# Two orders moved in a Strassen decoder trunk: where partial products are copied and finished in the second feed-forward entry, and in which order attention's two accumulators leave PSUM

## The chip, the cores and the metric

The kernel runs on one NeuronCore of one Trainium2 chip. The metric is the device time of one execution in microseconds. Smaller is better.

The engines are named as the profile names them: PE is TensorE's matrix multiply (PEld its weight loads), DVE is VectorE, ACT is ScalarE, POOL is GpSimd, and SP is SyncE, which issues most of the loads. Each of them works through its own list of instructions in order; an instruction that waits for a semaphore holds up everything behind it on the same engine.

## The reference

The program is a decoder trunk of two layers over 1024 positions and 1024 channels, all in float32. Layer 0 mixes by a short gated convolution, layer 1 by dilated attention with three branches; a SwiGLU feed-forward with 2816 hidden channels follows each. Cut to what matters here:

```
for i in range(2):
    h = rms_norm(x, mix_norm[i])
    x = x + (short_conv_mixer(h, ...) if i == 0 else dilated_attention_mixer(h, ...))
    h = rms_norm(x, ffn_norm[i])
    x = x + (silu(h @ w_gate[i]) * (h @ w_up[i])) @ w_down[i]
return rms_norm(x, final_norm)

# dilated attention: 16 heads of 64, q, k, v from one projection
s = q . k * 64**-0.5 + bias(distance), masked to the branch's band
o, lse = softmax(s) @ v, logsumexp(s)            # for each of three branches
o = sum(softmax(lse over branches) * o); x = x + o @ w_out
```

## The kernel before

**Precision.** A float32 operand is split into a high part (a copy rounded to the fast matmul type, made by ACT, line 139 or 567) and a low part (the rest, made by DVE, line 140 or 568). A product then takes three matmuls: high by high, high by low, low by high (lines 369 to 371 in plain products, 575 to 577 in the Strassen ones). Low parts of the weights are read by lines 371 and 577 alone.

**Feed-forward.** The gate and up projections are done by Strassen's scheme in Winograd's form: a unit `u` is one pair of 128-channel tiles, and instead of eight block products it takes seven, `(u, m)` with `m` from 1 to 7. Each product is 12 matmuls of 128x512. Gate units are even, up units odd. The order in which the products stand is a table (`unit_order`). In the second feed-forward (`key` 1) it begins `(0,1) (1,1) (2,1) (3,1) (0,2) (1,2) (2,2) (3,2) (4,1) (4,2) (0,6) (1,6) (0,7) (1,7) (0,4) (1,4) (0,5) (1,5) (0,3) (1,3) (2,6) (2,5) (2,7)`, numbered from 0, and goes on with units 3, 4 and so forth. One bank of PSUM, `p`, takes products 1, 6, 7 and 4 of a unit one upon the other; after 1, 6 and 7 ACT copies the bank out as a partial sum (line 581, tile `part`), and the next product of the unit must wait for that copy. Another bank, `r`, takes products 5 and 3; between the two DVE adds it to a saved partial (line 585). A third, `q`, holds product 2 until it is added to the saved product 1 (`first`, line 585). So the four quarters of a unit come out: `(0,0)` is the plain sum of products 1 and 2, the others need more. For a finished quarter ACT takes the SiLU (line 1239, gate units), DVE multiplies (line 1242, up units), POOL stores it.

**Operands of the second half.** The seven sums of activation blocks that the products read (tiles `b`) are made while the first products run, since they need the norm of the second 512 columns. `second_half` is a generator: each `next` makes one more piece. Its steps are: sums for product 7 and, at the following `next`, 6; a subtraction (`hcol<-hcol,x`); high and low parts for product 4, with a scaling (`x<-x,rstd`); a subtraction (`hcol<-x`); high and low parts for product 5 (`b<-hcol`); high and low parts for product 3 (`b<-x`). `start(n)` runs behind product number `n` and, at the numbers in a table, takes one such step after it has asked for the weights of product `n + 3` (`ensure`).

**Attention.** The heads are handled one a slot, 16 slots and one more to drain. Slot `n` computes the scores of head `n` (matmuls of line 1503 and 1504 into a fresh bank of PSUM each, read by DVE) and beside them the values of head `n - 1` (`values`, line 1579): small matmuls, in 14 pieces, into two accumulators, `acc[0]` for the first 512 positions and `acc[1]` for the second. ACT copies each accumulator out as 64 rows of denominators (`z`, line 1598) and 64 rows of outputs (`o`, line 1599). Dense projections of other heads are laid between. In odd slots ACT then splits the next pair's keys and queries (`split_kq`, line 1472), and at the end of each slot it takes the exponentials (line 1566; the first is tile `lf`), which the values of the next slot read. PSUM has 8 banks; a freed bank goes to the next one that asks, and the order of all instructions on each engine is fixed as the program is written.

**The end of attention.** For the last pair, `finish` turns the denominators into factors by logarithm and exponential, scales each half of the output and splits it, while `ensure` prepares the weights of the output projection (`ahead_ao` is the place of its third tile, counted from 0 as tile 2).

Of the kernel before, what the change touches and what calls it, by code (L numbers as in the profile page):

```python
# [24 lines left out]
NPAIR = H // 2  # L25
# [65 lines left out]
def view(t, off, dims):  # L91
    return bass.AP(tensor=t.tensor, offset=t.offset + off, ap=[t.ap[0]] + [list(d) for d in dims])
# [3 lines left out]
def trunk(ctx: ExitStack, tc: tile.TileContext, x, gains_in, cwi, ck, cwo, wqkv, wo, relb,  # L96
# [8 lines left out]
    def page(name, dt=F32):  # L105
        return pages.tile([128, 1024], dt, name=name, tag="page", bufs=PAGES)
# [6 lines left out]
    def bank():  # L113
        return psum.tile([128, 512], F32, name="bank", tag="bank")

    def half(h):
        return slice(h * HALF, (h + 1) * HALF)
# [45 lines left out]
    def ensure(upto):  # L163
        while op_state[0] < min(upto + 1, len(ops)):
            key = ops[op_state[0] + 1][0] if op_state[0] + 1 < len(ops) else None
            if key in sums_of:
                sums_of.pop(key)()
            if op_state[0] not in made:
                made[op_state[0]] = ops[op_state[0]][1]()
            op_state[0] += 1  # L170

    def take(key, ahead=1):
        i = op_state[1]
        assert ops[i][0] == key, (ops[i][0], key)
        ensure(i + ahead)
        op_state[1] += 1
        return made.pop(i)
# [196 lines left out]
    def run(*gens):  # L374
        for _ in zip(*gens):
            pass
        for g in gens:
            for _ in g:
                pass
# [6 lines left out]
    def both(w, ks, acts):  # L386
        banks = two_banks()
        run(product(w, ks, acts, banks))
        return banks
# [114 lines left out]
    def add_to_x(n, banks):  # L504
        for (c0, c1), b in banks.items():
            nc.vector.tensor_tensor(out=X[n][:, c0:c1], in0=X[n][:, c0:c1], in1=b[:, :c1 - c0], op=ALU.add)  # L506
# [34 lines left out]
    class Strassen:  # L541
# [75 lines left out]
        def whole(self, u, m, d):  # L617

            if m == 1:
                d["p"] = self.bank()  # L620
            elif m in (2, 5):
                d["q" if m == 2 else "r"] = self.bank()
            self.mm((u,), m, d["q" if m == 2 else "r" if m in (5, 3) else "p"], m in (1, 2, 5))
            if m in (1, 6, 7):
                d[{1: "u1", 6: "u2", 7: "u3"}[m]] = self.save(d["p"])
            if (u, m) == (0, 6):
                self.first(0)
            if m == 4:
                self.out(u, (1, 0), d.pop("p"))
            elif m == 3:  # L630
                self.out(u, (0, 1), self.add(d.pop("u2"), d.pop("r")))
            elif m in (5, 7) and "u3" in d and "r" in d:
                self.out(u, (1, 1), self.add(d.pop("u3"), d["r"]))
            early = self.key != 0
            if m == 2 and u > 3 + early or (u, m) in ((0, 4), (3, 7)):
                for x in {0: range(4), 3: (4,) * early}.get(u, (u,)):
                    self.out(x, (0, 0), self.first(x))
                    del self.st[x]["u1"]

# [506 lines left out]
    class Swiglu(Strassen):  # L1146
# [100 lines left out]
        def feed_forward(self, stats, last_step, after, final=None):  # L1247
            prep = []

            def start(n):  # L1250
                if n == 0:
                    last_step()
                    if not self.key:
                        for m in (6, 7):
                            combos[self.key, 1](m)
                        ensure(self.at(3, 1))
                if n == 1 + self.key:
                    next(stats)
                if n == 1:
                    if self.key:  # L1260
                        for m in (6, 7):
                            combos[self.key, 1](m)
                    ensure(self.at(0, 6))
                if n == 2 + 2 * self.key:
                    run(stats)
                    prep.append(self.second_half())
                    next(prep[0])
                    nc.scalar.activation(scratch, eps, AF.Silu)
                if n == 2:
                    ensure(self.at(1, 6))  # L1270
                elif n == 4:
                    ensure(self.at(1, 7))
                if n in ((5, 7, 8, 9, 11), (5, 6, 9, 10, 11, 15))[self.key]:
                    ensure(self.base + n + 3)
                    next(prep[0], None)

            self.run(start)
            key = ("d", self.key)
            if final:
                final(key, self.plain, self.hid)  # L1280
                return
            for n in range(KT):
                add_to_x(n, both(take(key + (n,)), self.plain, self.hid))
                after(n)
# [95 lines left out]
    def blk(j):  # L1380
        return (j // 4) * HALF + (j % 4) * 8

    def attention(norm):
# [185 lines left out]
        def values(p, a, st):  # L1569
            lf, lh, ld, lp = (st[n] for n in ("lf", "lh", "ld", "lp"))  # L1570
            o, z = st["o"], st["z"]
            n0 = slice(64 * a, 64 * a + 64)
            z0 = slice(64 - 64 * a, 128 - 64 * a)
            acc = [bank(), bank()]
            kd = [[128, 4], [1, 32]]
            b1 = [[32, 16], [1, 8]]

            def mm(ih, off, dims, u, rhs, first=False, last=False):
                nc.tensor.matmul(view(acc[ih], off, dims), vx[:, u, 64 * a:64 * a + 128], rhs,  # L1579
                                 start=first, stop=last)  # L1580

            for ih in range(2):
                for r4 in range(4):
                    mm(ih, r4 * 32, kd, 8 + r4, view(lf, ih * HALF + r4 * 32, kd), first=r4 == 0)
                    if r4 % 2:
                        yield
            for r4 in range(4):
                mm(1, r4 * 32, kd, 12 + r4, view(lh, r4 * 32, kd))
                if r4 % 2:
                    yield  # L1590
            for j in range(8):
                off = (j % 4) * 8
                mm(j // 4, off, b1, j, view(ld, blk(j), b1), last=False)
                if j:
                    mm(j // 4, off, b1, j - 1, view(lp, blk(j), b1), last=j % 4 == 3)
                if j % 4 == 3:
                    ih, s = j // 4, half(j // 4)
                    nc.scalar.activation(z[n0, s], acc[ih][z0], AF.Copy)
                    nc.scalar.activation(o[n0, s], acc[ih][n0], AF.Copy)
                yield  # L1600

        def finish(p):

            o, z = OZ.pop(p)
            if p < NPAIR - 1:
                zd, rd = zdram[p]
                nc.sync.dma_start(zd, z[0:65:64])
                yield
                zc = scope["pool"].tile([128, 16], F32, name="zc", tag="zc", bufs=2)
                nc.sync.dma_start(zc, bass.AP(zd.tensor, zd.offset, [[16, 128], [1, 16]]))  # L1610
                yield
                nc.vector.reciprocal(zc, zc)
                nc.sync.dma_start(bass.AP(rd.tensor, rd.offset, [[16, 128], [1, 16]]), zc)
                yield
                nc.sync.dma_start(z, bass.AP(rd.tensor, rd.offset, [[S, 2], [0, 64], [1, S]]))
                yield
                put_off.append((p, o, z))
                return

            acts[p] = page("o_hi", F32R), page("o_lo", F32R)  # L1620

            def scaled(c0, c1):
                q = slice(c0, c1)
                nc.vector.tensor_tensor(out=o[:, q], in0=o[:, q], in1=z[:, q], op=ALU.mult)

            def parts(h):
                split(o[:, half(h)], [t[:, half(h)] for t in acts[p]])

            nc.scalar.activation(z, z, AF.Ln)
            for h in range(2):  # L1630
                nc.scalar.activation(z[:, half(h)], z[:, half(h)], AF.Exp, scale=-1.0)
                scaled(h * HALF, h * HALF + HALF)
                parts(h)
                yield

        def attended():
# [27 lines left out]
        def slot(n, dense, ndense, late=0, hook=iter(())):  # L1664
# [40 lines left out]
            if a == 0 and p:  # L1705
                extra = finish(p - 1)
# [49 lines left out]
        ahead_ao = [k for k, f in ops].index(("ao", 1, 2))  # L1756
# [70 lines left out]
    with tc.tile_pool(name="first", bufs=1) as scope["pool"]:  # L1827
# [7 lines left out]
        def after(n):  # L1835
            if n in (0, 2):
                ensure(op_state[1] + 1)
            norm.add(n)
            nc.gpsimd.dma_start(spill[n], X[n])
            if n in (0, 2):  # L1840
                next(tab, None)
# [145 lines left out]
```

## Time and profile before

| what | value |
|---|---|
| median of 3 runs | 2145.89 us (2144.81 to 2146.08) |
| profiled execution | 2144.39 us |
| its span, first to last instruction | 2142.6 us |
| granted TensorE clock, mean over the span | 0.997 |
| PE busy | 2120.2 us, 99% |
| DVE busy | 1728.1 us, 81% |
| ACT busy | 1002.8 us, 47% |
| POOL busy | 221.9 us, 10% |

The convolution and the first feed-forward take about the first 990 us of the span. Attention lies between about 1010 and 1461 us, its output projection ends at 1489 us, and the second feed-forward follows to the end; its first products, the "second entry", start at 1489.48 us and, where nothing stops them, take 2.72 us each. A row of the timeline gives start and duration in us, engine, line, operation, out<-in tiles, shapes and how many were merged; in brackets stands the idle time of the engine before it and what ended it. Matmuls overlap: the start-to-start time tells the pace, the duration does not.

### The profile page before, as it was taken

The page shows a single profiled execution, that of the slowest core. Times are in us where ns is not written, and L with a number is a line of the kernel's source. Part 1 is how long each engine was busy: PE and PEld are TensorE (multiplying, and loading weights), DVE is VectorE, ACT ScalarE, POOL GpSimd, SP SyncE. Part 2 cuts the span into 40 slices and gives each one's busy share as a digit, 9 for nine tenths or more (in the row PEclk, how much of TensorE's full clock was granted, in tenths as well). Part 3 has the DMA queues.
Part 4 walks back from the last instruction along what each step waited for, and adds up shares of the span by engine and source line. Part 5 has one row for each costly group of instructions (what it writes and reads, how often), then busy time and mean ns, then how long its engine had stood idle before and what let it go on. Part 6 is the DMA issues. An engine that isn't in the chain of part 4 may idle for free.

```text
span 2142.6 us, 30734 instructions
## 1 busy us (share of the span) xinstructions
PE 2120.2 (99%) x11086; PEld 1816.1 (85%) x11086; DVE 1728.1 (81%) x3160; ACT 1002.8 (47%) x1798; POOL 221.9 (10%) x316
## 2 busy tenths in 40 slices
PE   9999999999999999999999999999899999999998
PEld 7788887888888888878999999887788888888887
DVE  8898669888888788864777777868888888978886
ACT  7433336344544444344555555536544444444435
POOL 2000001111212000010111111110011212100000
PEclk9999999999999999999999999999999999999999
DMA  7222643335545784331333333635114544586432
GB/s 214 69 93 69 236 147 94 114 123 172 168 154 181 267 305 141 107 135 52 92 93 94 93 95 83 204 119 185 44 69 156 184 157 166 172 333 217 155 94 79
DMA packets 148067, 306.71 MB, mean 143 GB/s; under 512 B 49851, under 2 KB 61131, under 8 KB 147915
## 3 DMA queue, kind: packets, MB, share of 16 engines
q1 hardware_dynamic: 82026, 206.83, 30.2%
q0 software_dynamic: 25872, 79.02, 10.5%
q10 hardware_dynamic: 40016, 18.90, 3.0%
q8 instruction: 88, 1.44, 0.3%
q14 instruction: 65, 0.52, 0.1%
HBM read 209.06 MB, written 88.28 MB: 139 GB/s over the span
## 4 chain that ended last, share of the span: by engine, by line
PE 77%; issue 10%; DVE 7%; ACT 4%; DMA 2%; POOL 0%; SPq 0%; ACTq 0%; DVEq 0%; POOLq 0%
PE bank L575 16%; PE bank L576 16%; PE bank L577 16%; PE bank L1579 4%; PE bank L371 4%; PE bank L369 4%; PE bank L370 4%; PE bank L670 2%; PE bank L673 2%; PE bank L672 2%; PE bank L1504 1%; PE bank L1503 1%; PE bank L1444 1%; PE bank L1443 1%; PE bank L1442 1%
## 5 line engine op out<-in xcount | busy, mean ns | idle before, releaser
L575 PE MATMUL bank<-b,w 128*128 128x512 f32 x1816 | 710.2, 391 | 6.8 <-ACT part L581 2.8
L576 PE MATMUL bank<-b,w 128*128 128x512 f32 x1816 | 708.1, 390 | 0.5 <-DVE b L916 0.5
L577 PE MATMUL bank<-b,w 128*128 128x512 f32 x1816 | 707.5, 390 | 0.8 <-DVE w L140 0.8
L575 PEld LDWEIGHTS bank<-b,w 128*128 128x128 f32 x1816 | 341.5, 188 | 80.4 <-ACT part L581 3.7
L577 PEld LDWEIGHTS bank<-b,w 128*128 128x128 f32 x1816 | 341.3, 188 | 73.1 <-DVE w L140 1.9
L576 PEld LDWEIGHTS bank<-b,w 128*128 128x128 f32 x1816 | 341.4, 188 | 70.8 <-DVE b L916 1.4
L139 ACT ACTIVATE w<-combo 128x512 fp32r<-128x512 f32 (+2 forms) x448 | 229.1, 540 | 248.6 <-DVE combo L191 227.3
L140 DVE TENSOR_TENSOR w<-combo,w 128x512 fp32r<-128x512 f32 (+2 forms) x448 | 254.8, 582 | 31.5 <-ACT w L139 31.2
L581 ACT ACTIVATE part<-bank 128x512 f32<-128x512 f32 x168 | 100.0, 597 | 294.9 <-PE bank L577 291.2
L140 DVE TENSOR_TENSOR w<-raw,w 128x512 fp32r<-128x512 f32 (+2 forms) x308 | 169.4, 569 | 21.8 <-ACT w L139 21.6
L585 DVE TENSOR_TENSOR part<-part,bank 128x256 f32<-128x256 f32 (+1 forms) x328 | 154.2, 501 | 37.9 <-ACT part L581 21.5
L139 ACT ACTIVATE w<-raw 128x512 fp32r<-128x512 f32 (+2 forms) x308 | 150.8, 527 | 63.2 <-DMA raw<-in_ffn_w_down 18.5
L831 DVE TENSOR_TENSOR x<-x,bank 128x512 f32<-128x512 f32 x168 | 114.8, 684 | 37.1 <-PE bank L577 34.5
L369 PE MATMUL bank<-w_hi,w 128*128 128x512 f32 (+1 forms) x320 | 119.6, 374 | 0.0
L371 PE MATMUL bank<-w_hi,w 128*128 128x512 f32 (+1 forms) x320 | 117.9, 369 | 1.3 <-DVE w L140 1.3
L370 PE MATMUL bank<-w_lo,w 128*128 128x512 f32 (+1 forms) x320 | 117.8, 368 | 0.0
L506 DVE TENSOR_TENSOR x<-x,bank 128x512 f32<-128x512 f32 (+1 forms) x104 | 66.0, 643 | 55.9 <-PE bank L371 48.6
L369 PE MATMUL bank<-h_hi,w_hi 128*128 128x512 f32 x256 | 104.5, 408 | 0.0
L191 DVE TENSOR_TENSOR combo<-raw 128x512 f32<-128x512 f32 (+1 forms) x160 | 103.2, 645 | 0.0
L371 PE MATMUL bank<-h_hi,w_lo 128*128 128x512 f32 x256 | 100.0, 391 | 0.2 <-DVE w_lo L140 0.2
L370 PE MATMUL bank<-h_lo,w_hi 128*128 128x512 f32 x256 | 99.9, 390 | 0.0
L1557 POOL PARTITION_ALL_REDUCE mb<-m x16 | 51.6, 3222 | 395.1 <-DVE m L1554 325.7
(266 smaller groups left out, 3804.4 us busy)
## 6 DMA issues: line engine op xcount, KB each, us to landing
hin<-part SPq DMA_DIRECT2D x126, 256.0 KB
raw<-in_ffn_w_gate SPq DMA_DIRECT2D x44, 512.0 KB
raw<-in_ffn_w_up SPq DMA_DIRECT2D x44, 512.0 KB
b<-ready SPq DMA_DIRECT2D x42, 512.0 KB
part<-sum POOLq DMA_DIRECT2D x72, 256.0 KB, 3.5
raw<-in_ffn_w_down SPq DMA_DIRECT2D x48, 384.0 KB
x<-spill SPq DMA_DIRECT2D x24, 512.0 KB
raw<-in_attn_w_qkv SPq DMA_DIRECT2D x24, 512.0 KB
```

The lines of the kernel that those rows point to most:

```text
L139: nc.scalar.activation(hi, src, AF.Copy)
L140: eng.tensor_tensor(out=lo, in0=src, in1=hi, op=ALU.subtract)
L191: eng.tensor_tensor(out=c, in0=a, in1=b, op=op)
L369: nc.tensor.matmul(b, whi[:, a], ahi[:, s], start=first, stop=False)
L370: nc.tensor.matmul(b, whi[:, a], alo[:, s], start=False, stop=False)
L371: nc.tensor.matmul(b, wlo[:, a], ahi[:, s], start=False, stop=last)
L575: nc.tensor.matmul(b, hi[:, a], bhi, start=start and k == 0, stop=False, skip_group_check=True)
L576: nc.tensor.matmul(b, hi[:, a], blo, start=False, stop=False, skip_group_check=True)
L577: nc.tensor.matmul(b, lo[:, a], bhi, start=False, stop=k == n - 1, skip_group_check=True)
L581: nc.scalar.activation(t, b, AF.Copy)
L585: nc.vector.tensor_tensor(out=t, in0=t, in1=b, op=ALU.add)
L831: nc.vector.tensor_tensor(out=X[n][:, half(h)], in0=X[n][:, half(h)], in1=b, op=ALU.add)
```

## The change

Four edits, in the second half of the program.

1. `whole`: in the second feed-forward the plain quarters `(0,0)` of units 0 to 3 are finished behind product `(1,3)`, where they were finished behind `(0,4)`. The other feed-forward and the convolution keep their place.
2. `start`: in the second feed-forward the steps of `second_half` that stood behind products number 9, 10, 11 and 15 stand behind 11, 12, 13 and 16.
3. `values`: for all pairs of heads but the last, both accumulators are copied at the end, `acc[1]` first and then `acc[0]`; before, `acc[0]` was copied after the fourth block of keys and `acc[1]` after the eighth.
4. `finish`: for the last pair, tile 3 of the output projection's weights is asked for between the first and the second half.

```
-            if m == 2 and u > 3 + early or (u, m) in ((0, 4), (3, 7)):
-                for x in {0: range(4), 3: (4,) * early}.get(u, (u,)):
+            if m == 2 and u > 3 + early or (u, m) in ((1, 3) if self.key == 1 else (0, 4), (3, 7)):
+                for x in {u * (u < 2): range(4), 3: (4,) * early}.get(u, (u,)):
                     self.out(x, (0, 0), self.first(x))
...
-                if n in ((5, 7, 8, 9, 11), (5, 6, 9, 10, 11, 15))[self.key]:
+                if n in ((5, 7, 8, 9, 11), (5, 6, 11, 12, 13, 16))[self.key]:
                     ensure(self.base + n + 3)
                     next(prep[0], None)
...
-                if j % 4 == 3:
-                    ih, s = j // 4, half(j // 4)
+                for ih in ((j // 4,) * (j % 4 == 3) if p == NPAIR - 1 else (1, 0) * (j == 7)):
+                    s = half(ih)
                     nc.scalar.activation(z[n0, s], acc[ih][z0], AF.Copy)
                     nc.scalar.activation(o[n0, s], acc[ih][n0], AF.Copy)
...
                 scaled(h * HALF, h * HALF + HALF)
                 parts(h)
+                if h == 0:
+                    ensure(ahead_ao + 1)
                 yield
```

How this moves instructions is shown at three places. PE's own list of matmuls is the same before and after.

The first place is ACT in slot 2 of attention, at the copies of the two accumulators of head 1 (`bank_9850` is `acc[0]`, `bank_9851` is `acc[1]`). Before:

```order
L139 ACTIVATE w_hi_9831<-raw_9509 128x1024 [waits DMAHW3_49]
L1598 ACTIVATE z_9546<-bank_9850 64x512 [waits PE_49]
L1599 ACTIVATE o_9545<-bank_9850 64x512
L1598 ACTIVATE z_9546<-bank_9851 64x512 [waits PE_49]
L1599 ACTIVATE o_9545<-bank_9851 64x512
```

and now:

```order
L139 ACTIVATE w_hi_9831<-raw_9509 128x1024 [waits DMAHW3_49]
L1598 ACTIVATE z_9546<-bank_9851 64x512 [waits PE_49]
L1599 ACTIVATE o_9545<-bank_9851 64x512
L1598 ACTIVATE z_9546<-bank_9850 64x512
L1599 ACTIVATE o_9545<-bank_9850 64x512
```

The four copies keep their place in ACT's list, but the first of them now waits for the last matmul of the values, where before the first pair waited only for the matmuls into `acc[0]`.

The second place is ACT in the second entry, behind the parts for product 6. Before:

```order
L567 ACTIVATE b<-x 128x512 x4
L581 ACTIVATE part<-bank 128x512
L567 ACTIVATE b<-hcol 128x512 x4
L581 ACTIVATE part<-bank 128x512 x2
L139 ACTIVATE w<-raw 128x512
L567 ACTIVATE b<-hcol 128x512 x4
L581 ACTIVATE part<-bank 128x512
L139 ACTIVATE w<-raw 128x512
L581 ACTIVATE part<-bank 128x512
L139 ACTIVATE w<-combo 128x512
L1239 ACTIVATE gate<-bank 128x512
```

and now:

```order
L567 ACTIVATE b<-x 128x512 x4
L581 ACTIVATE part<-bank 128x512 x3
L139 ACTIVATE w<-raw 128x512
L567 ACTIVATE b<-hcol 128x512 x4
L581 ACTIVATE part<-bank 128x512
L139 ACTIVATE w<-raw 128x512
L581 ACTIVATE part<-bank 128x512
L139 ACTIVATE w<-combo 128x512
L567 ACTIVATE b<-hcol 128x512 x4
L1239 ACTIVATE gate<-bank 128x512
```

The copies of products `(0,6)` and `(1,6)` now stand ahead of the four high parts for product 4, and those of `(0,7)` and `(1,7)` ahead of the high parts for product 5.

The third place is DVE in the same stretch, from the subtraction `hcol<-hcol,x` on. Before:

```order
L1187 TENSOR_TENSOR hcol<-hcol,x 128x512 x4
L568 TENSOR_TENSOR b<-hcol,b 128x512 x4
L1187 TENSOR_TENSOR x<-x,rstd 128x512 x4
L1187 TENSOR_TENSOR hcol<-x 128x512 x4
L140 TENSOR_TENSOR w<-raw,w 128x512
L568 TENSOR_TENSOR b<-hcol,b 128x512 x4
L140 TENSOR_TENSOR w<-raw,w 128x512
L140 TENSOR_TENSOR w<-combo,w 128x512
L1242 TENSOR_TENSOR part<-part 128x512
```

and now:

```order
L1187 TENSOR_TENSOR hcol<-hcol,x 128x512 x4
L140 TENSOR_TENSOR w<-raw,w 128x512
L568 TENSOR_TENSOR b<-hcol,b 128x512 x4
L1187 TENSOR_TENSOR x<-x,rstd 128x512 x4
L140 TENSOR_TENSOR w<-raw,w 128x512
L1187 TENSOR_TENSOR hcol<-x 128x512 x4
L140 TENSOR_TENSOR w<-combo,w 128x512
L568 TENSOR_TENSOR b<-hcol,b 128x512 x4
L191 TENSOR_TENSOR combo<-raw,combo 128x512
```

Low parts of weights now stand between the steps for the activations, and the work on the plain quarters (lines 585 and 1242) has moved behind them. From the first `hcol<-hcol,x` to the low part of the weights of product `(2,7)` both lists hold the same 52 instructions: 12 of line 1187, 12 of 568, 9 of 140, 7 of 191, 6 of 585, 5 of 1242 and 1 of 749. Behind that low part the lists are alike again.

## The prediction, made before the changed kernel ran

> **What bounds the kernel now.** The page's first part and the waits of PE come first.
>
> ```profile
> PE 2120.2 (99%) x11086; PEld 1816.1 (85%) x11086; DVE 1728.1 (81%) x3160; ACT 1002.8 (47%) x1798; POOL 221.9 (10%) x316
> ...
> PE bank L575 <- ACT part L581: 2.8, 2, 1.5
> PE bank L1503 <- ACT o L1599: 2.3, 4, 0.6
> PE bank L575 <- DVE part L585: 1.9, 1, 1.9
> PE bank L371 <- DVE w L140: 1.3, 2, 1.0
> ```
>
> PE is the bound everywhere, and its list of matmuls does not change, so only its waits can move the time. The four edits aim at these four rows. What such a wait costs is more than its idle time, and whether it goes depends on what ACT and DVE have queued. So I read the timeline at each place.
>
> **Edit 3, the accumulators.** Slot 2 of attention:
>
> ```profile
> 1068.94 1.41 DVE L1514 TENSOR_TENSOR lf<-bank,bias 128x256 f32<-128x256 f32 x4
> ...
> 1071.81 0.40 PE L370 MATMUL bank<-h_lo,w_hi 128*128 128x512 f32 x1
> 1072.04 0.40 PE L371 MATMUL bank<-h_hi,w_lo 128*128 128x512 f32 x1
> ...
> 1072.38 0.59 ACT L1599 ACTIVATE o<-bank 64x512 f32<-64x512 f32 x1
> ...
> 1073.02 0.39 PE L1503 MATMUL bank<-qa,ka 128*128 128x256 f32 x1 [0.58 <-ACT o L1599]
> ...
> 1073.25 0.28 PE L1504 MATMUL bank<-ql,ka 128*128 128x256 f32 x1
> ...
> 1073.36 0.28 PE L1503 MATMUL bank<-qa,ka 128*128 128x256 f32 x1
> ```
>
> The scores want a bank and get the one that the copies of `acc[0]` are just leaving. Matmuls of 512 columns follow each other by 0.23 us, so the scores were due at 1072.27 and started 0.75 late; the next one came after 0.23 instead of 0.11. One such wait costs 0.87 us, four cost 3.5. With `acc[0]` copied last, the scores must take another bank; the next that comes free is one that DVE reads for `lf`, done at 1070.35, two us before it is wanted. So I take the 3.5 as gone.
>
> The price is on ACT, in slot 1 and its like:
>
> ```profile
> 1044.91 0.59 ACT L1599 ACTIVATE o<-bank 64x512 f32<-64x512 f32 x1
> 1047.73 0.60 ACT L1598 ACTIVATE z<-bank 64x512 f32<-64x512 f32 x1 [2.23 <-PE bank L1579]
> ...
> 1047.73:1062.29 14.56, 14.56 (x110) 13.98 (x109) 11.72 (x15) 14.26 (x21) 3.23 (x1) 1.00 0.13 38
> ...
> 1062.29 1.05 ACT L1566 ACTIVATE lf<-lf 128x1024 f32<-128x1024 f32 x1
> ...
> 1063.62 1.05 PE L1579 MATMUL bank<-lf,vx 128*128 128x128 f32 x8
> ...
> 1105.93 0.63 ACT L1472 ACTIVATE qb<-kq 64x512 fp32r<-64x512 f32 x1 [1.39 <-POOL mb L1557]
> ```
>
> The first pair of copies ran in free time (2.23 us idle behind it). From 1047.73 to the exponential of `lf` ACT works without a stop (the windows row: its fourth count, 14.26 of 14.56 us in 21 instructions). Two copies more at its head, 0.60 + 0.59, push that exponential from an end at 1063.34 to 1064.53, and the values of the next slot, which read it and start at 1063.62 now, to 1064.58: 0.96 late, and 0.1 for the restart as above. So slot 1 pays 1.06. Slot 5 is alike:
>
> ```profile
> 1169.34 1.04 ACT L1566 ACTIVATE lf<-lf 128x1024 f32<-128x1024 f32 x1
> ...
> 1170.64 1.05 PE L1579 MATMUL bank<-lf,vx 128*128 128x128 f32 x8
> ```
>
> 1170.38 + 1.19 + 0.05 is 0.98 past 1170.64, so 1.08; I count slot 9 the same. In slot 3, as the last row of the fence ahead shows, ACT stands 1.39 us for POOL's maximum in the middle of the splits; that hole takes up the 1.19, and I count slots 7 and 11 like it, and slot 13 as free since no such value wait stands near it. Three times 1.07 is 3.2. Bounds: no slot pays (a gain of 3.5) to seven odd slots pay (3.5 - 7.5, a loss of 4.0). I take **a gain of 0.3**.
>
> **Edit 4, the weights of tile 3, and what comes behind.**
>
> ```profile
> 1425.46 0.69 DVE L506 TENSOR_TENSOR x<-x,bank 128x512 f32<-128x512 f32 x1 [6.86 <-DMA x<-spill]
> ...
> 1460.54 1.96 DVE L140 TENSOR_TENSOR w<-raw,w 128x384 fp32r<-128x384 f32 x4
> ...
> 1461.15 0.50 PE L371 MATMUL bank<-w_hi,w 128*128 128x512 f32 x1 [0.98 <-DVE w L140]
> 1461.48 0.40 PE L369 MATMUL bank<-w_hi,w 128*128 128x512 f32 x1
> ...
> 1471.25 0.69 DVE L506 TENSOR_TENSOR x<-x,bank 128x512 f32<-128x512 f32 x1 [0.75 <-PE bank L371]
> ...
> 1478.28 1.12 PE L501 MATMUL bank<-diag,ones 128*128 128x512 f32 x2
> ```
>
> PE waits for the first of four low parts at 1460.54. Moved between the halves it is ready two to three us sooner, and the wait goes: 0.98 idle, 0.16 hidden by the drawn duration (0.40 for a pace of 0.23) and 0.1 restart, 1.25 us. On the other side ACT's second exponential and DVE's second scaling come about 0.5 later; nothing of PE reads them before the first halves of all eight tiles are done. But PE needs DVE again at 1478.28, for the norm's diagonal, and DVE's only idle time on the way is the 0.75 at 1471.25. So no more than about **0.8** of the 1.25 survives. Bounds 0 to 1.25.
>
> Against it stands the x that DVE waits 6.86 us for. Odd slot 13 hands its two late copies on to the exponentials and to DVE, and what SP issues behind DVE's work, that x among it, is issued later by up to 1.19, less the holes on the way. PE does not wait there now, by how little no row tells. I take **a loss of 0.5** between 0 and 1.2.
>
> **Edits 1 and 2, the second entry.** Rows of ACT and PE, then four windows, whose counts are PE, PEld, DVE, ACT, POOL, then the granted clock (the last window holds DVE alone):
>
> ```profile
> 1523.62 2.42 ACT L567 ACTIVATE b<-hcol 128x512 fp32r<-128x512 f32 x4 [2.74 <-DVE hcol L1187]
> 1525.95 1.07 ACT L581 ACTIVATE part<-bank 128x512 f32<-128x512 f32 x2
> ...
> 1526.59 0.50 PE L575 MATMUL bank<-b,w 128*128 128x512 f32 x1 [1.31 <-ACT part L581]
> ...
> 1533.84 0.50 PE L575 MATMUL bank<-b,w 128*128 128x512 f32 x1 [1.52 <-ACT part L581]
> ...
> 1546.93 0.47 PE L575 MATMUL bank<-b,w 128*128 128x512 f32 x1 [1.87 <-DVE part L585]
> ...
> 1530.76:1534.17 3.41, 1.89 (x8) 1.24 (x8) 3.41 (x6) 3.30 (x6) 0.00 (x0) 1.00 0.00 0
> 1544.41:1547.82 3.41, 1.54 (x7) 0.98 (x6) 3.38 (x6) 1.64 (x3) 0.00 (x0) 1.00 0.06 23
> 1547.82:1551.23 3.41, 3.41 (x10) 2.64 (x9) 2.79 (x5) 0.78 (x2) 0.54 (x1) 0.50 0.00 0
> ...
> 1522.84:1558.32 35.48, 32.34 (x54) 0.95 0.09 37
> ...
> DVE w L140 <- ACT w L139: 1.3, 2, 0.7
> DVE part L585 <- PE bank L577: 0.9, 1, 0.9
> DVE part L1242 <- ACT part L1239: 0.5, 1, 0.5
> ...
> 1557.64 0.68 DVE L140 TENSOR_TENSOR w<-combo,w 128x512 fp32r<-128x512 f32 x1
> ...
> 1559.95 0.39 PE L577 MATMUL bank<-b,w 128*128 128x512 f32 x1
> ```
>
> The first two waits are copies of partials that stood on ACT behind four high parts, which themselves waited 2.74 us for DVE; the third is DVE's addition on bank `r` behind four low parts. All three should go with the new order: 1.31 + 1.52 + 1.87, with 0.26 each for drawn duration and restart, 5.5 us. The third cost more: behind it PE had a clock of 0.50 for 3.41 us, which loses half of it, 1.7. Together 7.2 us stand on this stretch.
>
> But DVE is almost full here, 32.34 of 35.48 us, and both orders hold the same 52 instructions up to the low part of the weights of `(2,7)` (54 with the two cut at the window's edges). That part ends at 1558.32 now, and PE reads it at 1559.95. So DVE decides how far PE can come forward. Its idle time of 3.14 loses one 0.7 (the weights behind high part 5), the 0.5 and the 0.9 (a slowed PE), and gains a new wait: the low part of a weight now stands first behind `hcol`, and ACT makes its high part only after the copies of `(1,6)`, whose matmuls end at 1525.28 (1526.59 - 1.31). One copy and one high part later, 0.6 each, is 1526.5, where DVE was free at 1525.3: 1.2. The end moves by -2.1 + 1.2 to 1557.4, PE can read at 1557.5 instead of 1559.95, and 0.1 goes for the restart: **a gain of 2.4**. The other 4.8 of the 7.2 come back as waits of PE before that point: for the bank `p` that the SiLU behind high part 5 frees, for the same bank of unit 1 on DVE, now that banks `q` of units 2 and 3 stay filled until `(1,3)`, for high and low part 3, and last and longest for the weights of `(2,7)`. Bounds: DVE's idle time stays as it is, 1.5; or all of it but the other 0.6 goes, 4.0.
>
> **The sum:** -0.3 - 0.8 + 0.5 - 2.4 = -3.0 us. The profiled execution took 2144.39 us, 2142.6 of them span, so the changed one would take 2141.4. The median of the runs shown is 1.5 above it, and the forecast for a median is 2145.89 - 3.0 = **2142.9 us**, 0.14% less. What a measurement of this kernel can tell from no change is about 0.2%, 4.3 us: below 2141.6 would be faster, above 2150.2 slower.
>
> **Rivals.** *All that is removed pays.* DVE's new wait does not come or PE does not read that late, edit 1 and 2 give their 4.0, edit 4 its 1.25, nothing is lost at x: -0.3 - 1.25 - 4.0 = -5.6, 2140.3 us. For it: three waits of one cause each. Against it: the 52 equal instructions and a DVE that is 91% busy. Chance 0.22.
>
> *The new wait halves the clock.* What is left of PE's waits gathers before `(2,7)`, some 1.8 us: the 4.8 above less 0.5, 0.9 and 1.4 for the three earlier ones and 0.2 for restarts, each an estimate from DVE's and ACT's 0.6 a piece. A wait of 1.52 in a window of 3.41 left the clock at 1.00, one of 1.87 was followed by 0.50 for 3.41 us. A wait between them may do it again, if it falls into one window: +1.7, so -1.3 and 2144.6 us. Chance 0.25. [...]
>
> *Attention pays in every odd slot.* One mechanism, ACT's gapless run, at 1.07 a slot: from four slots on edit 3 loses more than its 3.5, and from six on the whole change loses. Seven make 7.5 - 3.5 = +4.0; with -2.4 and -0.3 for the rest it is +1.3, 2147.2 us, slower than before. For it: the gapless rows. Against it: the 1.39 hole of slot 3. Chance 0.10.
>
> *The change does not do what it says* in edit 3: the scores would wait for another bank instead. The row of `lf` speaks against it; it would cost the 3.5 that I booked, so +0.5 in all and 2146.4. It stays within the chance of the forecast's upper end.
>
> **How the numbers follow.** Forecast 0.43, the rivals 0.22, 0.25 and 0.10. The forecast's own range is 2141.3 to 2144.3 (the bounds of 1.5 and 4.0 do not all fall to one side). With the faster rival below and the clock and attention above, the range that leaves out two in ten is 2140.0 to 2146.4. Faster by over 0.2%: 0.22 and a tenth of the forecast, 0.27. Slower by over 0.2%: only with more than one term at its worst end, 0.06. Within: 0.67.
>
> **What would show it.** The waits for `o` (line 1599) before line 1503 are gone; in their stead values of slots 2, 6 and 10 wait about 1 us each for the exponential of `lf`. No wait at tile 3 of the output projection, but a longer one for the diagonal behind it. The waits for line 581 are gone; small ones stand before `(0,5)`, `(1,5)` and `(0,3)`, a long one for DVE's line 140 at `(2,7)`; the clock stays at 1.00 in the second entry. I am wrong if line 1579 waits in all odd slots or none, if PE runs through `(2,7)`, or if the clock drops again.

## The result

| | median, us | from, to | executions |
|---|---|---|---|
| before | 2144.81 | 2143.47, 2146.31 | 15 |
| changed | 2140.94 | 2139.84, 2142.90 | 15 |

The ratio is 0.9983, with a 95% interval of 0.9976 to 0.9990: 3.9 us less, between 2.1 and 5.1. The forecast was 3.0 less, a median of 2142.9. The 2140.94 measured lie inside the range of 2140.0 to 2146.4, but below the forecast's own 2141.3; of the 2.0 us between 2142.9 and 2140.94, 1.1 is the median of before, 2144.81 here where three executions had given 2145.89. The move is 0.18%, so it stays just inside the 0.2% that was called no change. The profiled execution of the changed kernel took 2141.93 us, 2140.2 of them span.

The page's first row for the changed kernel:

```profile
PE 2118.5 (99%) x11086; PEld 1815.3 (85%) x11086; DVE 1719.1 (80%) x3160; ACT 1001.8 (47%) x1798; POOL 221.2 (10%) x316
```

PE is as full as before. The waits of PE (in total, times, longest):

```profile
PE bank L1579 <- ACT lf L1566: 2.4, 3, 0.8
...
PE bank L577 <- DVE w L140: 2.1, 3, 1.3
...
PE bank L575 <- DVE gate L1242: 0.7, 1, 0.7
...
PE bank L575 <- ACT b L567: 0.4, 1, 0.4
```

The waits for `o` (line 1599), for the copies of partials (line 581) and the long one for line 585 are gone. New are three waits of the values for the exponential of `lf`, and a row of smaller ones in the second entry. The timeline at the three places, first slot 2 of attention:

```profile
1065.02 1.05 ACT L1566 ACTIVATE lf<-lf 128x1024 f32<-128x1024 f32 x1
...
1066.13 1.16 PE L1579 MATMUL bank<-lf,vx 128*128 128x128 f32 x8 [0.82 <-ACT lf L1566]
...
1074.66 0.40 PE L371 MATMUL bank<-h_hi,w_lo 128*128 128x512 f32 x1
1074.90 0.28 PE L1503 MATMUL bank<-qa,ka 128*128 128x256 f32 x1
1075.02 0.28 PE L1504 MATMUL bank<-ql,ka 128*128 128x256 f32 x1
```

The scores follow the dense matmul by 0.24 us, with no wait; the values ahead of them wait. Then tile 3 of the output projection and the norm's diagonal behind it:

```profile
1461.62 0.39 PE L371 MATMUL bank<-w_hi,w 128*128 128x512 f32 x1
...
1471.57 0.69 DVE L506 TENSOR_TENSOR x<-x,bank 128x512 f32<-128x512 f32 x1
...
1478.60 1.12 PE L501 MATMUL bank<-diag,ones 128*128 128x512 f32 x2
```

PE doesn't wait at either, and DVE no longer waits ahead of the addition at 1471.57. Then PE's waits in the second entry:

```profile
1536.63 0.50 PE L575 MATMUL bank<-b,w 128*128 128x512 f32 x1 [0.15 <-ACT gate L1239]
...
1540.33 0.47 PE L575 MATMUL bank<-b,w 128*128 128x512 f32 x1 [0.66 <-DVE gate L1242]
...
1543.74 0.50 PE L575 MATMUL bank<-b,w 128*128 128x512 f32 x1 [0.45 <-ACT b L567]
1544.57 0.50 PE L576 MATMUL bank<-b,w 128*128 128x512 f32 x1 [0.32 <-DVE b L568]
...
1557.26 0.50 PE L577 MATMUL bank<-b,w 128*128 128x512 f32 x1 [1.25 <-DVE w L140]
```

They stand before `(0,5)`, `(1,5)`, `(0,3)` (two rows) and `(2,7)`. A window over DVE alone, from the first `hcol<-hcol,x` to the end of the low part that `(2,7)` reads (length, DVE's busy time, clock):

```profile
1523.15:1557.20 34.05, 31.98 (x54) 1.00 0.09 35
```

**Where the time went.** PE's list of matmuls is the same in both kernels, so the start of one and the same matmul in two traces can be subtracted. The values of slot 2 start at 1063.62 before and 1066.13 now, the tile-3 matmul at 1461.15 and 1461.62, the diagonal at 1478.28 and 1478.60, and the matmul of `(2,7)` at 1559.95 and 1557.26. In such a comparison the changed execution was already 1.5 us late when it came to the first changed place (2.51 at slot 2, of which 0.98 is its new wait). One place that makes up for most of that is this wait for a weight, far from all edits:

```profile
757.96 0.47 PE L575 MATMUL bank<-b,w 128*128 128x512 f32 x1 [0.76 <-ACT w L139]
```

The kernel before, in the second of its two further profiles (below), shows the same wait with 0.71. It is scatter, and a whole span can't tell a gain of 1 us from it. So the table below takes three stretches apart, each between the starts of two matmuls of the same number in both traces: attention (1062.2 to 1348.6 in the trace of before), tile 3 with the wait for x ahead of it and the diagonal behind it (1416.6 to 1517.4), and the second entry (1522.4 to 1563.1). It has all kernels of this document. Negative is shorter than in before's profile.

| kernel | attention | tile 3 | second entry | median, us | ratio to before | 95% interval |
|---|---|---|---|---|---|---|
| the change | -0.19 | -1.02 | -2.88 | 2140.94 | 0.9983 | 0.9976 to 0.9990 |
| edit 3 alone | -0.20 | -0.13 | -0.07 | 2143.08 | 0.9993 | 0.9983 to 1.0002 |
| edit 3, first heads alone | +3.16 | -0.27 | 0.00 | 2147.45 | 1.0010 | 1.0002 to 1.0019 |
| edit 4 alone | +0.03 | -0.08 | -1.57 | 2143.83 | 0.9993 | 0.9984 to 1.0002 |
| edits 1 and 2 | -0.05 | -0.39 | -2.83 | 2142.35 | 0.9988 | 0.9980 to 0.9997 |
| edit 1 alone | -0.07 | -0.12 | -2.29 | 2143.23 | 0.9994 | 0.9985 to 1.0003 |
| edit 2 alone | -0.07 | +1.07 | -1.85 | 2144.00 | 0.9997 | 0.9989 to 1.0006 |
| change, edit 3 for second heads | -3.43 | -1.62 | -2.88 | 2137.51 | 0.9969 | 0.9958 to 0.9980 |
| that, with quarters behind `(2,6)` | -3.43 | -1.28 | -4.42 | 2135.86 | 0.9963 | 0.9950 to 0.9977 |
| that, with other steps | -3.43 | -1.14 | -5.61 | 2134.65 | 0.9955 | 0.9942 to 0.9967 |
| before, again | -0.08 | -0.01 | -0.01 | (2144.56) | | |
| before, once more | -0.08 | +0.58 | +0.05 | (2146.22) | | |

The unchanged kernel shows what the stretches scatter by: 0.1 in attention, 0.6 at tile 3 (1.1 in edit 2 alone, which touches nothing there).

### The profile page after: what moved, and what is told of

The parts are those of the page before. It is cut to its first block, busy times and chain, and to the rows that moved or that the text cites. A ratio compares the mean times of both kernels' runs of the same rounds, so it can differ in the third digit from the quotient of the medians.

```text
span 2140.2 us, 30745 instructions
## 1 busy us (share of the span) xinstructions
PE 2118.5 (99%) x11086; PEld 1815.3 (85%) x11086; DVE 1719.1 (80%) x3160; ACT 1001.8 (47%) x1798; POOL 221.2 (10%) x316
## 4 chain that ended last, share of the span: by engine, by line
PE 76%; issue 10%; DVE 6%; ACT 5%; DMA 2%; POOL 0%; SPq 0%; ACTq 0%; DVEq 0%; POOLq 0%
PE bank L575 16%; PE bank L577 16%; PE bank L576 16%; PE bank L1579 4%; PE bank L371 4%; PE bank L369 4%; PE bank L370 4%; PE bank L670 2%; PE bank L673 2%; PE bank L672 2%; PE bank L1504 1%; PE bank L1503 1%; DVE w L140 1%; DVE combo L191 1%; DMA x<-spill 1%
## 5 line engine op out<-in xcount | busy, mean ns | idle before, releaser
L1598 ACT ACTIVATE z<-bank 64x512 f32<-64x512 f32 x32 | 19.0, 593 | 156.9 <-PE bank L1579 156.7
```

## The experiments

**Edit 3 alone.**

```
-                if j % 4 == 3:
-                    ih, s = j // 4, half(j // 4)
+                for ih in ((j // 4,) * (j % 4 == 3) if p == NPAIR - 1 else (1, 0) * (j == 7)):
+                    s = half(ih)
```

> Only the order of the accumulators' copies is changed (edit 3). Theory (ACT's gapless run): the four waits of the scores go (4 x 0.86 = 3.4 us), the values of slots 2, 6 and 10 wait for the exponential (3 x 1.06 = 3.2 us), so the time stays as before, -0.2 (between -0.8 and +0.4). Rival (the gain is edit 3's: waits removed pay, the new ones are drowned): -3.4. Rival (every odd slot pays): +3 to +4.

Attention became 0.20 shorter, as the first theory says. The median is 2143.08 beside 2145.07 us of before; the interval, 0.9983 to 1.0002, holds -0.2 as well as -3.4 us, so the verdict rests on the trace and on the next two kernels.

**Edit 3 for the first head of each pair alone**, whose copies fall in odd slots (`a` is the head's number in its pair):

```
-                for ih in ((j // 4,) * (j % 4 == 3) if p == NPAIR - 1 else (1, 0) * (j == 7)):
+                for ih in ((j // 4,) * (j % 4 == 3) if p == NPAIR - 1 or a == 1 else (1, 0) * (j == 7)):
```

> The new order of the copies for the first head of each pair alone, whose copies fall in the odd slots; the second heads keep the old order. Theory (the price is paid in odd slots, the gain made in even ones): the price alone, 3 x 1.06 = +3.2 us, with waits of the values in slots 2, 6 and 10 and the four waits of the scores still there. Rival (gain and price belong to the same slots): about 0.

The waits of PE:

```profile
PE bank L1579 <- ACT lf L1566: 2.4, 3, 0.8
PE bank L1503 <- ACT o L1599: 2.3, 4, 0.6
```

and the first of each kind in the timeline:

```profile
1064.96 1.16 PE L1579 MATMUL bank<-lf,vx 128*128 128x128 f32 x8 [0.81 <-ACT lf L1566]
1074.47 0.39 PE L1503 MATMUL bank<-qa,ka 128*128 128x256 f32 x1 [0.58 <-ACT o L1599]
```

Both kinds stand side by side: all of the price (+3.16), none of the gain. The median is 2.4 us above before, interval 0.4 to 4.1.

**The whole change, with edit 3 for the second head of each pair alone**, whose copies fall in even slots:

```
-                for ih in ((j // 4,) * (j % 4 == 3) if p == NPAIR - 1 else (1, 0) * (j == 7)):
+                for ih in ((j // 4,) * (j % 4 == 3) if p == NPAIR - 1 or a == 0 else (1, 0) * (j == 7)):
```

> The whole change, but the new order of the copies for the second head of each pair alone (even slots). Theory (gain in even slots, price in odd ones): the scores' four waits gone and the values' three waits gone, 3.2 us faster than the whole change, about -7.0 against before. Rival (gain and price are of the same slots): as the whole change, -3.9.

Attention is 3.43 shorter, with neither kind of wait left; at slot 2 the scores follow without a gap:

```profile
1072.26 0.40 PE L371 MATMUL bank<-h_hi,w_lo 128*128 128x512 f32 x1
1072.49 0.28 PE L1503 MATMUL bank<-qa,ka 128*128 128x256 f32 x1
```

The median is 2137.51 beside 2144.96 us, 7.4 less. So gain and price of edit 3 belong to different slots, and it had thrown its gain away in the odd ones.

**Edit 4 alone.**

```
                 parts(h)
+                if h == 0:
+                    ensure(ahead_ao + 1)
                 yield
```

> Only the request for the weights of tile 3 between the halves is changed (edit 4). Theory of the prediction: the wait of 1.25 us goes, DVE's idle 0.75 us ahead of the norm's diagonal lets 0.8 through: -0.8. Rival (what the profile of the whole change looks like): -1.1, nothing given back at the diagonal. Rival (DVE is late at the diagonal by all of it): 0, with the wait before the diagonal grown by 1.25 us.

Three rows of DVE and PE around tile 3:

```profile
1426.85 0.69 DVE L506 TENSOR_TENSOR x<-x,bank 128x512 f32<-128x512 f32 x1 [7.56 <-DMA x<-spill]
...
1461.55 0.39 PE L371 MATMUL bank<-w_hi,w 128*128 128x512 f32 x1
...
1478.91 1.13 PE L501 MATMUL bank<-diag,ones 128*128 128x512 f32 x2 [0.38 <-DVE diag L494]
```

The wait at tile 3 is gone. But x came later than in before's profile (DVE waited 7.56 us, there 6.86), which by the starts of the same matmuls cost PE 0.7 in the dense work behind it, and 0.38 of wait came up at the diagonal; the stretch ended with -0.08. Attention is unchanged here, so the late x isn't edit 3's doing. Over all profiles the stretch is shorter by 1.02, 0.08, 1.62, 1.28 and 1.14 in the five kernels with edit 4, mean 1.03, and longer by 0.09 on average in the eight without it (before's own counted as 0). Edit 4 is worth about 1.1 us, with a scatter as large as that in single executions. Most of the scatter is in the wait that it removes: between the matmuls that start at 1455.02 and 1464.93 in before's profile the five kernels with edit 4 are shorter by 1.10 (edit 4 alone) and 1.30 (the others), and the seven other profiles without it move by -0.59 to +0.92. The median, -1.2 us with an interval of -3.4 to +0.4, can't tell the three theories apart, and it has a part in it that belongs to the clock, below.

**Edits 1 and 2 alone** (their diff stands in the section on the change).

> Only the two edits of the second entry (1 and 2). Theory (DVE decides when PE may read the weights of product (2,7)): -2.4 to -3.0 us, granted clock 1.00 throughout the entry, a last wait of about 1.3 to 1.8 us for DVE's line 140 at (2,7). Rival (the whole of the change's gain comes from here): -3.9. Rival (the new wait halves the clock): -1.3.

The entry is 2.83 shorter, as in the whole change (2.88), with the same last wait:

```profile
1557.37 0.50 PE L577 MATMUL bank<-b,w 128*128 128x512 f32 x1 [1.28 <-DVE w L140]
```

The median is 2142.35 beside 2145.07 us, 2.7 less (0.6 to 4.3). By the stretch, and by a granted clock of 0.999 in the mean over the span (0.997 in before's profile), both rivals fall; the interval alone would not settle it.

**Edit 1 alone, and edit 2 alone.**

> Only the plain quarters are moved behind product (1,3) (edit 1); the steps of the second half stay. Theory (DVE decides, and the clock's share is real): the wait of 1.87 us before (0,3) goes and nearly all of it comes back before (2,7), because DVE's work up to that weight is the same; what stays is the half clock that followed that wait, so -1.7 us if the clock stays at 1.00. Rival (a wait of this size brings the half clock wherever it stands): a wait of some 1.7 us before (2,7), again followed by 0.50, and a time within 0.5 of before. Rival (removed waits pay): -3.7.

> Only the steps of the second half are moved (edit 2); the plain quarters stay behind (0,4). Theory (DVE decides): the waits for the copies of partials at (0,7) and (0,4) go, 3.3 us with their restarts, and come back before (1,5), some 2.3 us in two pieces, and before (0,3), which then has 1.8 to 2.3 us of wait in all: 0 if the half clock comes as before, up to -1.7 if it doesn't. Rival (removed waits pay): -3.3.

PE's waits behind `(1,4)` in the entry, first with edit 1 alone, then with edit 2 alone:

```profile
1558.45 0.50 PE L577 MATMUL bank<-b,w 128*128 128x512 f32 x1 [1.11 <-DVE w L140]
```

```profile
1542.72 0.50 PE L575 MATMUL bank<-b,w 128*128 128x512 f32 x1 [1.17 <-ACT w L139]
...
1544.13 0.50 PE L577 MATMUL bank<-b,w 128*128 128x512 f32 x1 [0.69 <-DVE w L140]
...
1548.23 0.51 PE L575 MATMUL bank<-b,w 128*128 128x512 f32 x1 [1.56 <-ACT b L567]
```

Two windows of edit 2 alone around these waits (PE, PEld, DVE, ACT, POOL, granted clock):

```profile
1541.96:1545.37 3.41, 1.97 (x7) 1.35 (x8) 3.31 (x7) 1.33 (x3) 1.01 (x3) 1.00 0.38 154
1545.37:1548.79 3.42, 1.81 (x7) 0.94 (x5) 3.38 (x6) 2.28 (x5) 0.15 (x1) 1.00 0.19 77
```

Edit 1 turns the 1.87 before `(0,3)` into 1.11 before `(2,7)`, where nearly all of it was expected to come back. Edit 2 turns the two waits for copies into others at the places that were named: 1.17 and 0.69 in `(1,5)`, where some 2.3 was expected, and 1.56 before `(0,3)` with 0.33 right behind it (not shown), where 1.8 to 2.3 was. So the waits moved as the theory says, and came back somewhat shorter. Edit 2 alone does not have the half clock (1.00 in both windows); nor, by its entry, has edit 1 alone (2.29 shorter, where -1.7 was expected if the clock stayed at 1.00, and a time within 0.5 of before if not). Of the 2.29 and 1.85 us the next experiment gives 1.57 to the clock, which leaves 0.7 for edit 1 and 0.3 for edit 2. In the medians they are -1.7 (-3.2 to +0.6) and -1.0 (-2.4 to +1.3).

**The kernel before, twice more.** The kernel with edit 4 alone has the old entry, with the old wait of 1.87, and yet its entry was 1.57 shorter. This is its wait:

```profile
1547.55 0.47 PE L575 MATMUL bank<-b,w 128*128 128x512 f32 x1 [1.87 <-DVE part L585]
```

and these are windows, the first two 3.41 us long, the last two around the next change of its clock:

```profile
1543.12:1546.53 3.41, 2.55 (x12) 1.78 (x10) 3.41 (x7) 1.91 (x4) 0.54 (x1) 1.00 0.29 117
1546.53:1549.94 3.41, 2.39 (x11) 1.99 (x12) 3.37 (x6) 1.78 (x3) 0.00 (x0) 1.00 0.00 0
...
1546.53:2137.03 590.50, 585.66 (x2990) 501.48 (x2990) 500.29 (x989) 265.67 (x537) 59.28 (x110) 1.00 0.47 160
2137.03:2140.44 3.41, 0.00 (x0) 0.00 (x0) 1.76 (x6) 0.00 (x0) 0.00 (x0) 0.50 1.03 357
```

The clock stayed at 1.00 through the same wait. In the profiles all changes of the clock within one execution lie whole multiples of 3.4133 us apart: in before the 583.68 us from 1551.23 (the end of the half clock that the prediction shows) to 2134.91 are 171 of them, in the execution of edit 3 alone the 1542.83 us from 7.87 to 1550.70 are 452. Counted back from 2137.03 by 173, a border of this execution lies at 1546.53, inside the wait, which runs from 1545.68 to 1547.55. It cuts it into 0.85 and 1.02. In before the wait lay whole between two borders. That gave the theory that was tried with the unchanged kernel:

> The kernel before, once more, for its clock in the second entry. Theory (the granted clock is set in steps of 3.41 us that start anew with each execution): 0.50 follows the wait of 1.87 us before (0,3) if that wait lies whole in one step, as in three of the profiles so far, and not if a border cuts it, as in one. Rival (the length of the wait decides): 0.50 follows in each.

> The same as the run before it, for one more execution: by the theory 0.50 follows in about (3.41 - 1.87) / 3.41 = 45% of the executions, by the rival in all.

The steps around the wait in the first and, below, the second of them:

```profile
1544.61:1548.02 3.41, 1.54 (x8) 0.98 (x7) 3.38 (x7) 1.31 (x3) 0.00 (x0) 1.00 0.15 62
1548.02:1551.44 3.42, 3.42 (x10) 2.65 (x9) 3.11 (x5) 1.10 (x2) 0.54 (x1) 0.50 0.00 0
```

```profile
1546.11:1549.52 3.41, 1.54 (x8) 0.97 (x7) 3.38 (x6) 1.62 (x3) 0.00 (x0) 1.00 0.01 1
1549.52:1552.93 3.41, 3.41 (x10) 2.64 (x9) 2.62 (x5) 0.63 (x1) 0.54 (x1) 0.50 0.00 0
```

The wait itself in the second:

```profile
1548.46 0.47 PE L575 MATMUL bank<-b,w 128*128 128x512 f32 x1 [1.87 <-DVE part L585]
```

Both times it lay whole in one step (from 1546.59 to 1548.46 in the second) and 0.50 followed. With the first profile of before and those of edit 4 alone, of edit 3 alone and of its first heads alone there are six of the old entry: five with the wait whole in a step and the half clock behind it (from 1547.82, 1548.02, 1549.52, 1550.70 and 1551.30), one with the wait cut and no half clock. The rival, that length alone decides, falls with that one. But length counts too: in all thirteen profiles 22 waits of PE between 1.1 and 1.58 us lay whole in a step (borders counted back by 3.4133 us), and 1.00 followed each. The longest is one of before, with its step and the one behind it:

```profile
61.26 0.47 PE L575 MATMUL bank<-b,w 128*128 128x512 f32 x1 [1.58 <-ACT w L139]
```

```profile
59.61:63.02 3.41, 1.83 (x9) 1.49 (x9) 3.38 (x6) 1.15 (x2) 0.00 (x0) 1.00 0.43 145
63.02:66.43 3.41, 3.41 (x17) 2.81 (x16) 3.38 (x6) 0.99 (x2) 0.00 (x0) 1.00 0.00 0
```

So of these waits within one step those of up to 1.58 us were followed by 1.00 and the five of 1.87 by 0.50; lengths between were not measured. The steps do not start with the kernel: in the six profiles the first border would lie 0.29, 1.05, 1.58, 1.65, 1.79 and 3.28 us behind the first instruction.

Five of six is more than the 45% that an even spread of borders gives; six are too few to say whether the spread is even. The mean granted clock gives a hint. It is 0.996 or 0.997 in the five profiles and 0.999 in the sixth. Of the 65 executions of the unchanged kernel with a recorded clock, 24 have 0.997 or less, 30 have 0.998 and 11 have 0.999. If those with 0.998 lack the half clock, about a third of the executions have it. This is not shown, since other steps at 0.50 lower the mean as well.

**A better version**, from the same reasoning. To the kernel with edit 3 for the second heads comes first another place for the plain quarters:

```
-            if m == 2 and u > 3 + early or (u, m) in ((1, 3) if self.key == 1 else (0, 4), (3, 7)):
-                for x in {u * (u < 2): range(4), 3: (4,) * early}.get(u, (u,)):
+            plain = (2, 6) if self.key == 1 else (0, 4)
+            if m == 2 and u > 3 + early or (u, m) in (plain, (3, 7)):
+                for x in range(4) if (u, m) == plain else {3: (4,) * early}.get(u, (u,)):
```

> The new order of the copies for the second heads alone, edits 2 and 4, and the plain quarters behind product (2,6) in place of (1,3); the steps of the second half as in the whole change. Theory (DVE's work ahead of the weights of (2,7) is what PE waits for there, and only that): the wait of 1.25 us before (2,7) goes, the waits of 0.15, 0.66, 0.45 and 0.32 ahead of it stay, one of some 0.4 us comes near 1576: about -8.6 against before, between the kernel of the even slots and the one with both tables moved. Rival (the waits ahead of (2,7) have the same cause and go too): -10.

The wait before `(2,7)` is gone and those ahead of it stay:

```profile
1535.93 0.47 PE L575 MATMUL bank<-b,w 128*128 128x512 f32 x1 [0.68 <-DVE gate L1243]
...
1539.34 0.50 PE L575 MATMUL bank<-b,w 128*128 128x512 f32 x1 [0.43 <-ACT b L567]
...
1540.17 0.50 PE L576 MATMUL bank<-b,w 128*128 128x512 f32 x1 [0.33 <-DVE b L568]
```

The entry is 1.54 shorter than without this (-4.42 for -2.88), and the median 2135.86 beside 2144.17 us, 8.3 less. Then the steps of the second half:

```
-                if n in ((5, 7, 8, 9, 11), (5, 6, 11, 12, 13, 16))[self.key]:
+                if n in ((5, 7, 8, 9, 11), (5, 6, 10, 12, 13, 15))[self.key]:
```

> As the run before it, and in the second entry the plain quarters behind product (2,6) and the steps behind products 10, 12, 13 and 15. Theory (DVE's work ahead of the weights of (2,7) is what PE waits for): with the plain quarters' additions and multiplications taken out from ahead of that weight the wait before (2,7) goes, the waits before (0,5) and (1,5) too, a wait of about 1.4 us before (0,3) and one of about 0.4 us near 1576 stay: about 3 us faster than the run before it, -10 against before. Rival (DVE is as late behind (2,7), so the wait only moves): as the run before it.

One wait of this kind is left in the entry:

```profile
1539.56 0.47 PE L575 MATMUL bank<-b,w 128*128 128x512 f32 x1 [1.22 <-DVE part L585]
```

The entry is 5.61 shorter than before's, and the median 2134.65 beside 2144.96 us: 0.9955 of before (0.9942 to 0.9967), 10.3 us less. It beats both kernels.

## Why the prediction was right, point by point

**Edit 3: -0.3 forecast, -0.19 in the trace.** The four waits of the scores went. Values waited in slots 2, 6 and 10 and in no other, as named, for 0.82, 0.79 and 0.79; a start late by 0.95 to 0.98 and a restart of 0.10 make 1.05 to 1.08 each, where 1.07 stood. The kernel with the first heads alone shows the price by itself (3.16 for 3.2), the one with the second heads the gain (3.43 for 3.5). The rival with every odd slot fell, and so did the one by which another bank is waited for.

**Edit 4: -0.8, with +0.5 for x; about -1.1 for both.** The wait went. Both terms were mis-sized. Of the wait 0.8 was to survive; the changed kernel gains 1.30 at it against before's profile and gives nothing back. The longer wait for the diagonal, one of the signs named, did not come; only the kernel with edit 4 alone shows it, with 0.38 of its 1.10. The forecast took the 0.75 us of idle time ahead of the addition at 1471.25 for all that DVE could give. That is gone in the changed kernel, but DVE made up 0.5 more ahead of tile 3, in its waits for ACT's high parts of weights between 1442 and 1449 (1.77 and 1.50 us before, 1.95 and 0.81 now). The loss at x was to be 0.5; PE lost 0.28 between the start of the stretch and tile 3, and not by edit 3. In the changed kernel DVE waited 7.18 us for x, and in the two other profiles of the unchanged kernel 7.01 and 7.06: it comes about as late without edit 3.

**Edits 1 and 2: -2.4 forecast, -2.88 in the trace.** The mechanism held: the waits for line 581 went, and PE waited again at the four places named, each for the engine and line named, but for less: 0.15, 0.66, 0.77 (0.45 + 0.32) and 1.25 where 0.5, 0.9, 1.4 and 1.8 were estimated. DVE decided: from the first `hcol<-hcol,x` to the low part for `(2,7)` it needed 34.05 us where it had needed 35.48. Its new wait, forecast as 1.2, came as such:

```profile
1526.85 0.69 DVE L140 TENSOR_TENSOR w<-raw,w 128x512 fp32r<-128x512 f32 x1 [1.21 <-ACT w L139]
```

DVE's idle time is 2.07, forecast 3.14 - 2.1 + 1.2 = 2.24; the rest of the difference is in the work itself, 31.98 for 32.34. PE read at 1557.26 instead of the 1557.5 forecast, and 0.32 of that is a delay it brought along. So the gain was under-sized by 0.5.

**What the forecast had wrong in this stretch** is whom it holds for. It took the half clock behind the wait of 1.87 for a part of the kernel before, and compared with an execution that had it. Of six profiles of the old entry five have it; against the one without, edits 1 and 2 gain 2.88 - 1.57 = 1.3. The median over many executions mixes the two, and by the hint from the mean clocks those without may be the majority.

**The rival of the new wait.** The granted clock was 1.00 in the entry (the window from 1521 to 1565). The wait before `(2,7)` was estimated at 1.8 us and came as 1.25, less than the 1.52 that had left the clock at 1.00. It lay whole in one step, so no border cut it; it is one of the 22 waits of up to 1.58 us that 1.00 followed:

```profile
1554.34:1557.75 3.41, 2.16 (x10) 1.50 (x9) 3.38 (x7) 1.72 (x4) 1.08 (x2) 1.00 0.49 197
```

The condition that a wait must fall into one window was named in the forecast; that the 1.87 of before itself meets it in some executions only, the one profile could not show. The steps run apart from the kernel's instructions: in the two further profiles of the unchanged kernel the border behind the wait lies 1548.02 and 1549.52 us from the first instruction, 1.5 apart, while the wait itself moved by 1.0.

**All that is removed pays** fell too, though its 1.25 for edit 4 came (1.30 at the wait): in the entry 2.88 is not 4.0, and edit 1 and edit 2 alone show the waits coming back.

**The sum.** -0.2, -1.0 and -2.9 make -4.1 in the traces of three stretches, -3.0 was forecast and -3.9 measured. That 4.1 comes so near 3.9 proves little: it holds against an execution with the half clock; against one without it the sum would be 2.5, and the interval of 2.1 to 5.1 holds both. That 3.0 lies in it too is partly luck: the loss at x, the gain at tile 3 and the gain in the entry were each off by 0.2 to 0.5, all three towards a larger gain, while the half clock that the forecast counted on in every execution pulls the other way.

## What to carry to other kernels

When an edit takes a wait away and puts one elsewhere, look whether both are in the same turn of the loop: here the gain was in even slots and the price in odd ones, and doing the edit in the even ones alone gave all of it. Where an engine that is almost full has to finish a given list of work before the bound engine can go on (here DVE, busy for 32.34 of 35.48 us), reordering the list moved waits about and gained little, 1.3 us against the execution without the half clock; taking work out of the list, here the plain quarters to behind that point, gained 1.54 more. Compare the starts of the same instruction in two traces, stretch by stretch: a span's scatter of 1 to 3 us hides a term that the stretch of attention shows to 0.1 (tile 3 scatters by 0.6 even so). And where a wait may or may not be followed by a slower clock, one profile of the kernel before is not enough to price it: here the same 1.87 us came with 1.57 more in one execution and without it in another.

## What was not expected of the hardware

That it matters how a wait lies against the steps of the clock was not expected, as told above. Two more places show that it isn't PE's idle time alone that brings 0.50. In the kernel with the quarters behind `(2,6)` eight small matmuls of the bias tables, with PE busy throughout, fell whole into one step:

```profile
936.34 2.59 PE L524 MATMUL bank<-oh,rel 33*16 33x512 f32 x8
```

```profile
935.71:939.12 3.41, 3.41 (x13) 1.16 (x12) 2.68 (x4) 1.89 (x2) 0.55 (x1) 1.00 0.18 74
939.12:942.53 3.41, 3.41 (x9) 2.63 (x9) 3.41 (x6) 1.49 (x2) 0.51 (x1) 0.50 0.40 109
```

The step behind it ran at 0.50. In the twelve other profiles the borders, counted back from the next change of the clock, cut these eight (at most 2.53 of their 2.59 us in one step), and 1.00 followed. What in them works like idle time is not shown. And the execution of edit 3 alone was 3.9 us behind that of before at 16 us: PE waited 1.04 us for the high part of an activation, where before's only wait of that kind is 0.42, and two steps at 0.50 came, the first from 7.87 on, inside that wait:

```profile
8.30 0.80 PE L575 MATMUL bank<-b,w 128*128 128x512 f32 x1 [1.04 <-ACT b L915]
```

```profile
4.46:7.87 3.41, 1.93 (x9) 0.99 (x8) 1.44 (x2) 1.37 (x3) 0.00 (x0) 1.00 0.99 336
7.87:11.28 3.41, 2.98 (x6) 2.10 (x7) 3.00 (x5) 2.81 (x5) 0.00 (x0) 0.50 1.06 406
11.28:14.70 3.42, 3.42 (x9) 2.65 (x9) 0.84 (x2) 1.80 (x4) 0.00 (x0) 0.50 0.97 328
```

Its PE was busy for 1.93 us of the step ahead, while the step with 1.81 in edit 2 alone (1545.37 to 1548.79) was followed by 1.00. So no threshold in PE's busy time, as the profile models it, fits all steps; what the clock looks at stays open.
